# Rows of scales by a DRAM store and a broadcast load in place of a matmul with ones

## The chip, the cores and the metric

The kernel runs on one core of one Trainium2 chip. Its time is the device time of one execution in microseconds, median over runs of the same kernel on the same chip. Inside a core, TensorE (PE) does matmuls, VectorE (DVE) and ScalarE (ACT) work element by element on 128 partitions, and the queues of SyncE (SP) and GpSimd (POOL) issue the transfers between DRAM and the on-chip memory. Each queue is in order: an instruction that waits holds all that stands behind it on the same queue.

## The reference

One encoder layer for two token groups that share the weights: the "sample" (1024 tokens) and the "prompt" (512 tokens), width 2048. Cut to what matters here:

```python
h = rms_norm(x, norm_g)                 # x * rsqrt(mean(x*x) + eps) * g, one scale for each token
z = h @ w_in                            # combined projection, 5632 columns
c_val, c_glu, c_gate, q, k, v, a_gate = split(z)
u = depthwise_conv31(c_val * sigmoid(c_glu)) + b_dw
u = silu(layer_norm(u, ln_g, ln_b))     # (u - mean) * rsqrt(var + eps): one scale for each token
conv_out = (u @ w_pw) * silu(c_gate)    # the "pointwise" product
attn_out = banded_attention(rope(q), rope(k), v, sink) * silu(a_gate)
y = rms_norm(x + concat(conv_out, attn_out) @ w_out, final_norm_g)
```

All is float32. On the chip a token's values lie along one row (the free direction), and the channels lie on the partitions. A scale for each token is therefore needed as a row of 512 numbers that is the same in all 128 partitions, while the sums that it comes from arrive as columns: 512 tokens stand as a tile of 128 partitions by 4.

## The kernel before

Every product runs as float32 split into a high and a low part (three matmuls for each block of 128x128 weights and 512 tokens). The sample's input and output projections use seven products of half-size blocks in place of eight (class `Unit` and `Onto`, line 207); the prompt's projections and both pointwise products are plain (`Job`, line 670). Each `Job` or `Unit` loads 512 KB weight blocks on SP (`raw`), ACT and DVE split them into `hl` (lines 510, 511, or 418, 420 where the low part comes from DRAM), and PE multiplies. At most three `raw` and three `hl` tiles exist.

Side work is written as generators that are queued on three lanes (`conv`: the taps of the convolution; `attn`: attention; `prep`: everything that prepares a later product). After each group of three matmuls the lanes are given `3 * MM` = 648 ns of credit times their rate. A generator does a step, and the number that it yields is the credit that must be earned before its next step. A `yield 6000` is thus a pause of ten groups of three matmuls when the rate is 1, which it is for the `prep` lane at the four places of the change. `drain` and `until` run a lane's remaining steps at once. The compiler layer below orders the instructions of each engine by priority and by the times that it estimates, so an instruction's place on its queue follows from the place at which it is written, from its priority and from that estimate.

Between column and row stands `Encoder.spread` (lines 726 to 743). It splits the 128x4 columns into high and low (lines 731, 732), builds two 128x512 tiles with four scaled copies of the identity each (line 737, eight instructions on DVE), pauses S8 = 6000, and sums over the partitions with two matmuls against a 128x128 tile of ones (line 742). The caller then copies the result from PSUM on ACT. It is used at eight places in time:

- twice in `spread_rms` (sample's RMS scale) and twice in `Mix.finish` (final norm of the sample);
- once in `scale_ahead`: the prompt's RMS scale `rcol`, computed by `rms_ahead` just before with a pause of 15000 behind it. The row `r` then multiplies the prompt's input (line 928), which goes to DRAM as `xr_d` and is loaded much later by `load_two`, when the prompt's projections begin;
- once in each of three `Post.prepare`: two for the halves of the sample's tokens, one behind the other on the `prep` lane, followed by `fetch` of the first half, and one for the prompt (`LastPost`). The scale `r` of the layer norm comes from `column_sums` and `rsqrt` (lines 701 to 724, then a pause S7 = 6000); its row `rs` multiplies the tiles (line 1489), then a SiLU (line 1492). The halves store the result to `cs_d` (line 504) and `fetch` loads it again (line 1513) and splits it (line 510, tile `t<-f`); the prompt's half keeps it and `split` does the same in the last `Onto` unit.

The tile `rs` is `bc[:, 1]` of a T1 tile (F tile for the prompt); `r` of `scale_ahead` is one of four G tiles. The two diagonal tiles of `spread` are two of the four U tiles.

Of the kernel before, what the change touches and what calls it, by code (L numbers as in the profile page):

```python
# [7 lines left out]
F32 = mybir.dt.float32  # L8
F32R = mybir.dt.float32r
AF = mybir.ActivationFunctionType  # L10
# [3 lines left out]
P = 128  # L14
# [25 lines left out]
LOAD = 4500  # L40
LEAD = 9000
SPREAD = 3
RATES = (0.4, 0.6, 0.3, 1.0, 0.5)
S1, S2, S3, S4, S5, S6, S7, S8 = 5000, 6000, 9000, 7000, 3500, 2500, 6000, 6000
NF, NA, NG, NU, NP = 7, 4, 4, 4, 4
# [385 lines left out]
class Encoder:  # L431
# [284 lines left out]
    def rsqrt(self, out, v, b):  # L716
# [6 lines left out]
        nc.vector.tensor_scalar(t, t, -0.5, 1.5, ALU.mult, ALU.add)  # L723
        nc.vector.tensor_tensor(out, s, t, ALU.mult)

    def spread(self, cols, b=NB, room=None):

        nc = self.nc
        hi = self.work.tile([P, b], F32R, tag="tinyr", bufs=4, name=self.name("tinyr"))
        lo = self.small(b)  # L730
        nc.vector.tensor_copy(hi, cols)
        nc.vector.tensor_tensor(lo, cols, hi.bitcast(F32), ALU.subtract)
        parts = []
        for part in (hi.bitcast(F32), lo):
            dg = (room or self.U)([b * P], F32R)
            for j in range(b):
                nc.vector.tensor_scalar(dg[:, j * P : (j + 1) * P], self.ident, part[:, j : j + 1], None, ALU.mult)
            parts.append(dg)
        yield S8
        ps = self.PS("s", [b * P])  # L740
        for n, dg in enumerate(parts):
            nc.tensor.matmul(ps, self.ones_r, dg, start=n == 0, stop=n == 1)
        return ps


class Sequence:
# [169 lines left out]
    def scale_ahead(self):  # L916

        e, nc = self.e, self.e.nc
        ps = yield from e.spread(self.rcol)
        r = e.G()  # L920
        nc.scalar.activation(r, ps, AF.Copy)
        yield 3000
        for i, dst in enumerate(self.xr_d):
            t = e.F([2, self.T])
            nc.sync.dma_start(t, self.xT[2 * i : 2 * i + 2].rearrange("k p t -> p k t"))
            yield 3000
            for j in range(2):
                nc.vector.tensor_tensor(t[:, j], t[:, j], r, ALU.mult)
            e.store(dst, t)
            yield 1500  # L930
# [507 lines left out]
class Post:  # L1438
# [9 lines left out]
    def prepare(self):  # L1448
        e, nc, seq, t0, N = self.e, self.e.nc, self.seq, self.t0, self.N
        cols = slice(t0, t0 + N)  # L1450
        bc, vs = self.room(), self.room()
        mu, rs, va = bc[:, 0], bc[:, 1], vs[:, 0]
        sq = (bc[:, 1], vs[:, 1])
        pairs = []
        for i in range(0, NC, 2):
            t = self.room()
            for j in (0, 1):
                nc.sync.dma_start(t[:, j], seq.conv_d[i + j][:, cols])
            pairs.append(t)
        xc = [pairs[i // 2][:, i % 2] for i in range(NC)]  # L1460
        both = lambda row: row.unsqueeze(1).broadcast_to([P, 2, N])
        yield 2 * LOAD
        nc.vector.tensor_tensor(vs, pairs[0], pairs[1], ALU.add)
        for t in pairs[2:]:
            nc.vector.tensor_tensor(vs, vs, t, ALU.add)
            yield 1500
        nc.vector.tensor_tensor(va, va, vs[:, 1], ALU.add)
        yield S3
        ps = yield from e.sums(va)
        nc.scalar.activation(mu, ps, AF.Copy, scale=1.0 / C)  # L1470
        yield 1000
        for i, t in enumerate(pairs):
            nc.vector.tensor_tensor(t, t, both(mu), ALU.subtract)
            for j in (0, 1):
                n = 2 * i + j
                nc.scalar.activation(sq[j] if n else va, t[:, j], AF.Square)
                if n:
                    nc.vector.tensor_tensor(va, va, sq[j], ALU.add)
            yield 2500
        yield S3  # L1480
        v = e.column_sums(va, N, 1.0 / C, LN_EPS)
        r = e.small(NB)
        e.rsqrt(r, v, NB)
        yield S7
        ps = yield from e.spread(r)
        nc.scalar.activation(rs, ps, AF.Copy)
        yield 1000
        for i, t in enumerate(pairs):
            nc.vector.tensor_tensor(t, t, both(rs), ALU.mult)
            for j in (0, 1):  # L1490
                n = 2 * i + j
                nc.scalar.activation(t[:, j], t[:, j], AF.Silu, scale=e.ln_g[:, n : n + 1], bias=e.ln_b[:, n : n + 1])
            self.normed(i, t)
            yield 3000
# [380 lines left out]
def encoder(ctx, tc, a):  # L1875
# [103 lines left out]
    def pace(unit, rate, lane=e.conv):  # L1979
        unit.before.append(lambda: setattr(lane, "rate", rate))  # L1980
# [9 lines left out]
    rms = sample.spread_rms()  # L1990
    for step in range(SPREAD):
        stages[0][-1].after.setdefault(step, []).append(lambda: e.urgently(next, rms, None))

    pace(stages[1][0], RATES[0])
    pace(stages[2][0], RATES[1])
    pace(stages[3][0], RATES[2])

# [47 lines left out]
    pace(end, 0.0)  # L2045
    pace(pj[2], RATES[3])

# [4 lines left out]
    def prepare():  # L2052
# [5 lines left out]
        for group in prompt.groups:  # L2058
            e.attn.add(group)

    pj[PM].before.append(prepare)
    pace(pj[PM], RATES[4])
    jobs = sum(items, []) + [[j] for j in pj]
# [114 lines left out]
```

## Time and profile before

| | us |
|---|---|
| median of 3 runs | 2078.28 (2077.58 to 2078.65) |
| profiled execution, its own time | 2079.13 |
| its span in the profile | 2077.4 |
| PE busy | 2060.1 |
| DVE busy | 1728.4 |
| ACT busy | 1081.8 |
| mean granted TensorE clock | 0.998 |

The span is the time between the first and the last instruction in the trace; the execution's own time is 1.73 us longer. "Busy" is the time in which the engine had at least one instruction under way. In the rows of a timeline the columns are the start in us, the length in us, the engine, the source line, the operation, the tiles written and read, and how many instructions were merged into the row; in square brackets stands the idle time before it and what ended it. In the chain of waits a row is start, length, and the engine and line on which the end depended at that time.

### The profile page before, as it was taken

What the parts mean: (1) busy time and instruction counts of PE and PEld (TensorE: products, weight loads), DVE (VectorE), ACT (ScalarE), POOL (GpSimd) and SP (SyncE); (2) the same over time, 40 slices, a digit from 0 to 9 for tenths busy, and PEclk for the clock granted to TensorE, in tenths of its full rate; (3) what the DMA queues carried; (4) which work ended last, traced back from release to release, by engine and by line L of the source; (5) the groups of instructions that cost most, each with busy time, mean ns of one, the idle gap of its engine ahead of it and who ended that gap; (6) DMA issues with size and microseconds to landing.
All of it is one profiled execution on the core that took longest, in us unless ns stands there. A gap on an engine that the chain in (4) does not pass through costs nothing.

```text
span 2077.4 us, 27223 instructions
## 1 busy us (share of the span) xinstructions
PE 2060.1 (99%) x9256; PEld 1697.9 (82%) x9256; DVE 1728.4 (83%) x2843; ACT 1081.8 (52%) x1771; POOL 157.9 (8%) x240
## 2 busy tenths in 40 slices
PE   9999999999999999999999999999999999999998
PEld 8888888888888888788888888888888887888886
DVE  8768899998899899889766777776799978998877
ACT  7486445333465555655555777336553343454454
POOL 0111111111112111100000000000000111100000
PEclk9999999999999999999999999999999999999999
DMA  8888886864577777954555555997789898778897
GB/s 285 309 300 256 200 215 226 286 218 158 190 243 197 181 167 179 279 167 158 164 183 185 178 172 188 316 329 233 239 295 295 279 324 283 213 259 277 293 324 279
DMA packets 242300, 494.56 MB, mean 238 GB/s; under 512 B 23664, under 2 KB 84464, under 8 KB 242160
## 3 DMA queue, kind: packets, MB, share of 16 engines
q1 hardware_dynamic: 216352, 428.83, 62.1%
q0 software_dynamic: 24512, 61.88, 12.5%
q10 hardware_dynamic: 1296, 2.11, 0.3%
q8 instruction: 72, 1.18, 0.2%
q14 instruction: 68, 0.56, 0.1%
HBM read 331.77 MB, written 160.96 MB: 237 GB/s over the span
## 4 chain that ended last, share of the span: by engine, by line
PE 73%; issue 8%; DMA 8%; DVE 7%; ACT 2%; POOL 1%; SPq 0%; ACTq 0%; POOLq 0%; DVEq 0%
PE a L207 21%; PE a L670 13%; PE c L207 10%; PE b L670 6%; PE c L670 6%; PE b L207 5%; PE s L1169 2%; PE pv L1198 2%; PE a L1852 2%; PE s L207 2%; DVE hl L511 2%; PE pt L1203 1%; PE s L1852 1%; DVE t L511 1%; DMA p<-y_d 1%
## 5 line engine op out<-in xcount | busy, mean ns | idle before, releaser
L207 PE MATMUL a<-t,hl 128*128 128x512 f32 x2640 | 632.5, 390 | 1.8 <-ACT u L236 1.3
L207 PEld LDWEIGHTS a<-t,hl 128*128 128x128 f32 x2640 | 493.5, 188 | 108.4 <-ACT u L236 2.4
L511 DVE TENSOR_TENSOR hl<-raw,hl 128x1024 fp32r<-128x1024 f32 (+3 forms) x334 | 337.8, 1012 | 151.5 <-ACT hl L510 147.3
L510 ACT ACTIVATE hl<-raw 128x1024 fp32r<-128x1024 f32 (+3 forms) x334 | 296.8, 889 | 314.4 <-PE c L207 88.1
L670 PE MATMUL a<-t,hl 128*128 128x512 f32 x1344 | 326.3, 393 | 0.0
L207 PE MATMUL c<-t,hl 128*128 128x512 f32 x1320 | 319.1, 389 | 0.0
L670 PEld LDWEIGHTS a<-t,hl 128*128 128x128 f32 x1344 | 248.8, 188 | 50.4
L207 PEld LDWEIGHTS c<-t,hl 128*128 128x128 f32 x1320 | 247.4, 188 | 51.5 <-DVE u L304 0.2
L1041 DVE SCALAR_TENSOR_TENSOR f<-f,c_w_dw,f 128x512 f32<-128x512 f32 x248 | 172.9, 744 | 0.2
L670 PE MATMUL b<-t,hl 128*128 128x512 f32 x672 | 162.9, 392 | 1.5 <-DVE t L515 0.8
L670 PE MATMUL c<-t,hl 128*128 128x512 f32 x672 | 163.9, 393 | 0.0
L1004 DVE SCALAR_TENSOR_TENSOR f<-f,c_w_dw,f 128x512 f32<-128x512 f32 x232 | 163.4, 742 | 0.2
L207 PE MATMUL b<-t,hl 128*128 128x512 f32 x660 | 159.8, 389 | 0.0
L670 PEld LDWEIGHTS b<-t,hl 128*128 128x128 f32 x672 | 124.8, 188 | 27.5 <-DVE t L515 1.1
L670 PEld LDWEIGHTS c<-t,hl 128*128 128x128 f32 x672 | 124.6, 188 | 24.8
L207 PEld LDWEIGHTS b<-t,hl 128*128 128x128 f32 x660 | 123.7, 188 | 25.6
L1033 DVE SCALAR_TENSOR_TENSOR f<-f,w_both,f 128x512 f32<-128x512 f32 x120 | 89.8, 748 | 2.0
L236 ACT ACTIVATE u<-a 128x512 f32<-128x512 f32 x82 | 48.8, 595 | 77.3 <-PE a L207 70.6
L236 ACT ACTIVATE g<-a 128x512 f32<-128x512 f32 x78 | 46.5, 596 | 78.5 <-PE a L207 68.5
L1183 ACT ACTIVATE p<-p,tiny 128x384 f32<-128x384 f32 (+1 forms) x96 | 54.6, 570 | 45.9 <-DVE tiny L1180 36.2
L510 ACT ACTIVATE a<-pt 128x512 fp32r<-128x512 f32 x64 | 38.0, 593 | 64.6 <-PE pt L1203 64.4
L285 POOL DMA_DIRECT2D g<-xT_s x16 | 8.8, 551 | 743.1 <-DMA att_d<-u 669.0
(356 smaller groups left out, 2765.2 us busy)
## 6 DMA issues: line engine op xcount, KB each, us to landing
raw<-w_in SPq DMA_DIRECT2D x170, 512.0 KB, 5.2
raw<-w_out SPq DMA_DIRECT2D x31, 512.0 KB, 5.1
raw<-w_pw SPq DMA_DIRECT2D x24, 512.0 KB, 4.2
wsum_P<-raw SPq DMA_DIRECT2D x47, 256.0 KB, 3.6
raw<-wsum_P SPq DMA_DIRECT2D x18, 512.0 KB, 5.1
f<-x_s SPq DMA_DIRECT2D x16, 512.0 KB, 8.5
g<-wsum_P SPq DMA_DIRECT2D x28, 256.0 KB, 4.6
a<-sum_S SPq DMA_DIRECT2D x24, 256.0 KB, 6.1
```

What stands on the lines that cost most here:

```text
L207: nc.tensor.matmul(acc, hl[:, l, o, j, :], toks[j][:, r], start=name in FRESH and j == 0 and q == 0, stop=name in LAST and j == HALF - 1 a ...
L236: nc.scalar.activation(t, bank, AF.Copy)
L510: nc.scalar.activation(hi, x, AF.Copy)
L511: nc.vector.tensor_tensor(lo, x, hi.bitcast(F32), ALU.subtract)
L670: nc.tensor.matmul(job.acc[0], hl[:, l, kk // HALF, kk % HALF, :], r, start=i == 0 and p == 0, stop=i == nk - 1 and p == 2,)
L1004: nc.vector.scalar_tensor_tensor(t, h[:, j : j + T], w(j), t, ALU.mult, ALU.add)
L1033: nc.vector.scalar_tensor_tensor(m0, odd[:, j : j + H], both(j), m0, ALU.mult, ALU.add)
L1041: nc.vector.scalar_tensor_tensor(out, d[:, j : j + H], w(2 * j + k), out if j else m0, ALU.mult, ALU.add)
L1169: nc.tensor.matmul(ps[:, 0:n], qs[:, x, h], k[y][:, keys], start=p == 0, stop=p == 2)
L1183: nc.scalar.activation(p[:, 0:n], p[:, 0:n], AF.Exp, bias=nm[:, h : h + 1], accum_out=l[:, h : h + 1])
L1198: nc.tensor.matmul(pv, v[x][:, vs], pt[:, y], start=i == 0 and p == 0, stop=i == last and p == 2)
L1852: nc.tensor.matmul(acc[t], self.toks[name, m][:, x, i, t * P : (t + 1) * P], parts[i][l].rearrange("p a b -> p (a b)"), start=fresh and fi ...
```

## The change

A new method `spread_far` takes a destination tile and the columns. It stores the 128x4 columns to a DRAM row of 512 numbers, pauses FAR = 6000, loads the row back into all 128 partitions with one broadcast transfer, and pauses FAR again. Both transfers are issued on SP. Two callers use it: `scale_ahead` (once) and `Post.prepare` (three times). In both the split, the eight scaled identities, the pause S8, the two matmuls and the copy from PSUM are gone. In `scale_ahead` the G tile is now taken ahead of the store. `spread_rms` and `Mix.finish` keep `spread`.

```diff
+FAR = 6000
...
+    def spread_far(self, dst, cols):
+        b = cols.shape[1]
+        row = self.tc.dram_tile([1, b * P], F32, name=self.name("row"))
+        self.store(row.rearrange("o (j p) -> p (o j)", p=P), cols)
+        yield FAR
+        self.nc.sync.dma_start(dst, row.broadcast_to([P, b * P]))
+        yield FAR
...
     def scale_ahead(self):
 
         e, nc = self.e, self.e.nc
-        ps = yield from e.spread(self.rcol)
         r = e.G()
-        nc.scalar.activation(r, ps, AF.Copy)
+        yield from e.spread_far(r, self.rcol)
         yield 3000
...
         e.rsqrt(r, v, NB)
         yield S7
-        ps = yield from e.spread(r)
-        nc.scalar.activation(rs, ps, AF.Copy)
+        yield from e.spread_far(rs, r)
         yield 1000
```

## The prediction

> **What bounds the kernel.** I read the page's busy line first, then busy time by stretch for PE alone, then PE's own waits.
>
> ```profile
> PE 2060.1 (99%) x9256; PEld 1697.9 (82%) x9256; DVE 1728.4 (83%) x2843; ACT 1081.8 (52%) x1771; POOL 157.9 (8%) x240
> core 0: us, PE busy (x), PEclk, DMA share, GB/s
> 350.00:420.00 70.00, 70.00 (x311) 1.00 0.74 259
> 1160.00:1300.00 140.00, 139.93 (x662) 1.00 0.57 185
> 1300.00:1420.00 120.00, 118.73 (x532) 1.00 0.89 308
> 1420.00:1800.00 380.00, 378.64 (x1716) 1.00 0.84 276
> 1800.00:1860.00 60.00, 60.00 (x269) 1.00 0.75 239
> sum 2077.40, PE 2060.05; mean PE 257.51
> ```
>
> PE is busy for all but 17.3 us of the span. The three stretches in which the change lies (350 to 420, 1160 to 1300, 1800 to 1860) hold 0.07 us of idle PE between them, at the full granted clock. So what the change takes off PE is time won, one for one, and what it takes off other engines is worth nothing unless PE waits for them. From 1160 to 1860 PE idles 0.07 + 1.27 + 1.36 = 2.70 us; more than that can't be won there by better feeding.
>
> **The matmuls that go.** Four of the eight calls of `spread` go, two matmuls each. The chain of waits runs over PE at three of the places and gives each matmul's share of the path; at the third place the PE timeline does.
>
> ```profile
> 359.56 2.72 PE b L207 x12
> 371.13 0.46 PE s L742 x2
> 1180.06 0.23 PE s L742
> 1181.55 0.24 PE s L742
> 1280.11 0.62 PE L742 MATMUL s<-u,ones_r 128*128 128x512 f32 x2
> 1280.57 0.86 PE L670 MATMUL c<-t,hl 128*128 128x512 f32 x3
> 1819.34 0.23 PE s L742
> 1820.03 0.29 PE s L742
> ```
>
> They cost 0.46 + 0.23 + 0.24 + (1280.57 - 1280.11 = 0.46, the 0.62 being overlapped by the next) + 0.23 + 0.29 = 1.91 us. An ordinary matmul of the same shape takes 2.72 / 12 = 0.227, and eight of them 1.81. I take the middle, 1.85 us. This is the only term with a sure place on the path.
>
> **DVE and ACT work that goes.** For each place two small instructions and eight scaled identities on DVE, one copy on ACT:
>
> ```profile
> 1270.47 0.16 DVE L731 CAST tinyr<-tiny 128x4 fp32r<-128x4 f32 x1
> 1270.67 0.88 DVE L737 TENSOR_SCALAR u<-c_ident,tinyr 128x128 fp32r<-128x128 f32 x4
> L1486 ACT ACTIVATE t<-s x2: 577/587/597, 1181.8 to 1281.1; 128x512 f32<-128x512 f32 x2
> ```
>
> The two DVE rows come once for the high and once for the low part: 2 x (0.16 + 0.88) = 2.08 us of DVE and 0.59 of ACT, 8.3 and 2.4 over the four. The stretches above show PE full there, so I cost this gain at nothing. Its upper bound is the 0.07 us idle in them; with later stretches, the third rival.
>
> **What is added on SP: the store.** It waits for the last instruction of `rsqrt`, as line 731 did before. What then stands behind it on SP are weight loads and stores. When `r` was ready in the first place and in the last, and the first instruction of the old `spread` in the first:
>
> ```profile
> 350.32 0.16 DVE L724 TENSOR_TENSOR stat<-tiny,tiny 128x4 f32<-128x4 f32 x1
> 364.59 0.16 DVE L731 CAST tinyr<-stat 128x4 fp32r<-128x4 f32 x1
> 1812.28 0.17 DVE L720 RECIPROCAL tiny<-tiny 128x4 f32<-128x4 f32 x1
> 1816.06 0.16 DVE L724 TENSOR_TENSOR tiny<-tiny,tiny 128x4 f32<-128x4 f32 x1
> SPq L504 <- DVE hl L511: 28.1, 7, 11.0
> ```
>
> In the first place `r` is 14 us early and SP waits for nothing. In the last one DVE put other work into `rsqrt`, which ran from 1812.28 to 1816.22; if SP gets there when that chain begins, it waits 3.9 us. The last row (SP's waits from 360 to 425) says what such a wait is worth: SP stood 11.0 us at one store, in a stretch in which PE lost nothing. So: 0 taken, and PE's loss is bounded by the slack of the weights, below.
>
> **The load.** It waits until the store has landed. Ahead of it lies a pause of 6000, ten ticks of three matmuls, 10 x 3 x 0.227 = 6.8 us. No transfer of before writes 4-byte pieces. The nearest rows of the issues (line, KB, median us to landing):
>
> ```profile
> wsum_P<-raw SPq DMA_DIRECT2D x47, 256.0 KB, 3.6
> xr_d<-f SPq DMA_DIRECT2D x8, 512.0 KB, 7.1
> a<-msum_S SPq DMA_DIRECT2D x12, 256.0 KB, 6.7
> ```
>
> `wsum_P<-raw` writes 128 partitions x 4 pieces of a 512-wide row, the store's pattern of 512 pieces with more bytes in each: 3.6 us. The slowest store is 7.1. I take 3.6 as the nearest, so the load finds it landed; at 7.1 SP stands 0.3 us. The load brings 256 KB into 128 rows like `a<-msum_S`, a slow one of its size: 6.7 us, under the second pause of 6.8 us, so DVE finds its row there; the 1000 or 3000 of credit that follow are kept besides.
>
> **What moves.** At each place two pauses of 6000 replace one, so the rest of the `prep` lane is written 6000 (6.8 us) later, after both halves' preparation 12000 (13.6 us, more where attention fills in). Who needs it, and when:
>
> ```profile
> L928 DVE TENSOR_TENSOR f<-f,g x16: 672/674/683, 380.3 to 422.2; 128x512 f32<-128x512 f32 x16
> L2015 SPq DMA_DIRECT2D a<-xr_d x6: 319/320/327, 605.5 to 846.3; - x6
> 1341.42 1.16 ACT L510 ACTIVATE t<-f 128x512 fp32r<-128x512 f32 x2 [4.48 <-DMA f<-cs]
> 1436.00 5.61 PE L670 MATMUL b<-t,hl 128*128 128x512 f32 x24
> 1838.14 1.51 ACT L1492 ACTIVATE f<-f,c_conv_ln_b,c_conv_ln_g 128x512 f32<-128x512 f32 x2
> 1848.77 0.61 ACT L510 ACTIVATE t<-f 128x512 fp32r<-128x512 f32 x1
> 1866.64 5.60 PE L670 MATMUL b<-t,hl 128*128 128x512 f32 x24
> ```
>
> The prompt's scaled input is finished about 7 us after 422 and loaded from 605.5 on. The sample's first half is split by 1342, then by about 1356; its first matmul is at 1436. The tightest is the prompt: its last SiLU ends at 1839.65, then at 1846.5, its split begins at 1848.77 and its first pointwise matmul at 1866.64. That leaves 2.3 us to the split and 18 to PE. All costed at 0 for this reason. The G tile held some 12 us longer and the two U tiles freed at each place stand against each other; PE's fullness hides both.
>
> **Sum.** The profiled execution took 2079.13 (span 2077.4 and 1.73 around it), 0.85 above the median. Less 1.85 it is 2077.28; on the median 2078.28 - 1.85 = 2076.4. The new order of the queues will move PE's few idle places by some tenths either way. I say 2076.5, 0.09% below before; a measurement of this kernel can tell about 0.2% (4.2 us) from no change, so this is "the same".
>
> **First rival: later traffic in a full stretch.** From 1300 to 1420 the DMA share is 0.89 at 308 GB/s, and PE already loses 1.27 us there:
>
> ```profile
> f<-cs SPq DMA_DIRECT2D x8, 512.0 KB, 5.9
> 1373.95 6.69 DVE f L1004 x11
> 1383.44 5.97 DMA a<-ag_d
> ```
>
> DVE works off eleven taps in a row, a gate of the attention lands late, and the operands of the next scores are late behind both. The change moves loads and stores of `cs` (512 KB each, 524288 / 308000 = 1.7 us of all engines) 13.6 us later into that stretch. For it: only 0.57 of the DMA is busy in the stretch that they leave. Against: they are 1 to 3 transfers, spread over 50 us. One to three in the way of that chain give 2078.2 to 2081.6.
>
> **Second rival, the slow side: SP stands at the load.** If 512 single-number pieces land far later than 3.6 us, SP stands at the load's wait and the weights come late. How long PE is covered, at the third place:
>
> ```profile
> 1280.57 1.22 DVE L511 TENSOR_TENSOR hl<-raw,hl 128x1024 fp32r<-128x1024 f32 x1 [2.79 <-DMA raw<-w_in]
> 1285.95 1.55 PE L670 MATMUL a<-t,hl 128*128 128x512 f32 x6
> DMA to landing us min/median/max: 3.7/5.6/9.1
> ```
>
> The `hl` for the job that starts at 1285.95 is ready at 1281.79, 4.2 us of slack. PE pays from a landing of 6.8 + 4.2 = 11 us on, which exceeds the slowest weight load around (9.1). At twice that, 18.2 us, SP stands 11.4, PE loses 7.2 at a place: 2083.7 for one, 2090.9 for two. Against it stand all rows of stores above.
>
> The Trainium skill, in "DMA: Bandwidth & Descriptors", speaks for this rival: "Rules for kernel authors" says that a last dimension that isn't contiguous becomes one descriptor for each element, and "Specifications" that pieces under 512 B are done as read-modify-write. By that rule the store's 4-byte pieces could each cost more than the 512-byte ones of `wsum_P<-raw`; by the row they cost no more. No run here shows 4-byte writes.
>
> **Third rival: the feeding gets better too.** With DVE relieved and the order changed, the idle time behind the second place, 2.70 us, may go as well: 2076.4 - 2.7 = 2073.7. Against: none of the waits there names the work that is removed.
>
> **How the numbers follow.** My forecast (2075.0 to 2078.2) 62%, the first rival 17%, the second 10%, the third 11%. Faster by over 0.2% means below 2074.1: nearly all of the third rival, 0.10. Slower by over 0.2% means above 2082.4: the second and a small part of the first that comes with more transfers, 0.12. The rest, 0.78, lies between. The range reaches from a little below the third rival, 2073.0, to the edge of the first, 2082.0; it leaves out the second.
>
> **What would show it.** Line 742 with 8 matmuls in place of 16, PE's busy time lower by about 1.8 and its idle time near 17.3. The store's landing near 3.6 us and no long wait of SP for the row. Lines 928 and 1489 without idle DVE ahead of them. `t<-f` of the first half near 1356 and the prompt's last SiLU near 1846. I am wrong if SP's waits show the row with more than 4 us at a place, if PE's idle time from 1300 to 1420 grows, or if it falls below 15 us in all.

## The result, and the profile after

The changed kernel takes 2104.81 us, median of 4 runs (2101.38 to 2107.92), against 2077.93 (2075.00 to 2078.65) before: the ratio is 1.013, with a 95% interval of 1.0113 to 1.0146. It is 27 us slower; 2076.5 was forecast. The profiled execution took 2107.08 us with a span of 2105.3.

The line of busy times of the changed kernel, and its busy time of PE by stretch (columns: stretch, its length, PE busy with the number of matmuls, granted clock, DMA share, GB/s):

```profile
PE 2067.0 (98%) x9248; PEld 1701.2 (81%) x9248; DVE 1723.3 (82%) x2803; ACT 1079.5 (51%) x1767; POOL 157.6 (7%) x240
```

```profile
350.00:420.00 70.00, 70.00 (x311) 1.00 0.82 255
1160.00:1300.00 140.00, 134.47 (x628) 0.98 0.54 152
1300.00:1440.00 140.00, 131.17 (x563) 0.96 0.88 301
1440.00:1820.00 380.00, 377.08 (x1712) 1.00 0.84 276
1820.00:1880.00 60.00, 53.60 (x230) 0.94 0.71 191
1184.00:1192.00 8.00, 2.47 (x10) 0.81 0.66 198
1192.00:1196.00 4.00, 4.00 (x14) 0.53 0.70 216
1856.00:1860.00 4.00, 0.34 (x1) 0.74 0.70 218
1860.00:1864.00 4.00, 4.00 (x10) 0.50 0.73 236
1864.00:1868.00 4.00, 4.00 (x17) 0.90 0.44 140
```

The eight matmuls are gone (9256 to 9248), and yet PE is busy 6.9 us longer, and the span is 27.9 longer. So there are two losses. PE's idle time rose from 2077.4 - 2060.1 = 17.3 to 2105.3 - 2067.0 = 38.3, by 21.0. And PE's busy time rose by 6.9 although 1.85 us of work left it, so that the same matmuls took 8.75 us longer. The last five rows show how: behind each gap the granted clock is 0.5 for a while.

The idle time sits at three places, none of them the first one (350 to 420 is full): 5.53 us up to 1300, 8.83 from 1300 to 1440, 6.40 from 1820 to 1880. Before, these stretches and the one from 1440 to 1820 had 0.07, 1.27, 0 and 1.36.

What SP, DVE and PE waited for in the changed kernel (engine, line, what it waited for: us in all, times, longest):

```profile
SPq L732 <- DMA row<-tiny: 27.8, 3, 11.5
```

```profile
DVE t L1496 <- DMA t<-row: 9.1, 2, 7.1
DVE f L1496 <- DMA f<-row: 6.6, 1, 6.6
```

```profile
PE a L208 <- DVE u L305: 6.9, 2, 6.4
PE pv L1206 <- DVE a L512: 5.9, 2, 5.5
PE s L1177 <- ACT a L511: 3.6, 1, 3.6
```

Line 732 is the broadcast load, 1496 the first multiplication by the loaded row. PE names neither: its longest waits are for DVE work of attention (512) and of the output projection (305); the 3.6 us for line 511 lie in the stretch from 1300 on. The link is in the chain of waits at the second and the fourth place (start, length, what), and in DVE's and PE's timelines:

```profile
1171.77 12.68 DMA row<-tiny
1184.47 4.92 DMA t<-row
1189.41 0.06 DVE t L1496
1190.56 0.70 DVE a L512
1191.30 1.22 PE pv L1206 x2
1836.12 11.65 DMA row<-tiny
1847.84 3.95 DMA f<-row
```

```profile
1189.41 1.23 DVE L1496 TENSOR_TENSOR t<-t,t 128x1024 f32<-128x1024 f32 x1 [7.15 <-DMA t<-row]
1851.81 1.23 DVE L1496 TENSOR_TENSOR f<-f,f 128x1024 f32<-128x1024 f32 x1 [6.61 <-DMA f<-row]
```

```profile
1191.30 1.22 PE L1206 MATMUL pv<-a,t 128*128 128x512 f32 x2 [5.53 <-DVE a L512]
1859.66 5.36 PE L208 MATMUL a<-t,hl 128*128 128x512 f32 x12 [6.40 <-DVE u L305]
```

The store of 512 single numbers lands after 12.68 and 11.65 us. SP issues the load only then, the load takes 4.9 and 3.95, and DVE, which goes through its instructions in order, stands 7.15 and 6.61 us in front of the multiplication. Behind it on DVE stood work that PE needed. And the twelve matmuls at 1859.66 took 5.36 us, where the prediction showed 2.72 for twelve.

### The profile page after: what moved, and what is told of

It reads as the page before. It is cut to its first block, busy times and chain, and to the rows that moved or that the text cites. A ratio compares the mean times of both kernels' runs of the same rounds, so it can differ in the third digit from the quotient of the medians.

```text
span 2105.3 us, 27176 instructions
## 1 busy us (share of the span) xinstructions
PE 2067.0 (98%) x9248; PEld 1701.2 (81%) x9248; DVE 1723.3 (82%) x2803; ACT 1079.5 (51%) x1767; POOL 157.6 (7%) x240
## 4 chain that ended last, share of the span: by engine, by line
PE 73%; DMA 8%; issue 8%; DVE 7%; ACT 2%; POOL 1%; SPq 0%; ACTq 0%; POOLq 0%; DVEq 0%
PE a L208 20%; PE a L671 11%; PE c L208 10%; PE c L671 6%; PE b L671 5%; PE b L208 5%; PE s L1177 2%; PE pv L1206 2%; PE s L1859 2%; DMA a<-ag_d 2%; PE a L1859 2%; PE s L208 2%; DVE hl L512 2%; PE pt L1211 1%; DMA row<-tiny 1%
## 5 line engine op out<-in xcount | busy, mean ns | idle before, releaser
L671 PEld LDWEIGHTS b<-t,hl 128*128 128x128 f32 x672 | 126.1, 190 | 27.9 <-DVE t L516 1.1
L512 DVE TENSOR_TENSOR a<-pt,a 128x512 fp32r<-128x512 f32 x64 | 44.0, 688 | 33.0 <-ACT a L511 32.2
```

Source lines behind the costliest of these rows:

```text
L512: nc.vector.tensor_tensor(lo, x, hi.bitcast(F32), ALU.subtract)
L671: nc.tensor.matmul(job.acc[0], hl[:, l, kk // HALF, kk % HALF, :], r, start=i == 0 and p == 0, stop=i == nk - 1 and p == 2,)
```

## The experiments

Each kernel was run alternately with the kernel before on the same chip. The theories, with a letter each: shift (S), the later writing of the `prep` lane alone; queue (Q), SP stands at the load and what is behind it comes late; DVE (D), DVE stands in order at the row; contention (C), the store of tiny pieces holds up the core's other transfers; order (O), the new order of instructions by itself. S and O have nothing to do with the transfers' lengths, Q, D and C have. In the expectations W stands for Q and D together, and O3 for O at the second half alone.

| run | edit | us | ratio (95%) |
|---|---|---|---|
| e1 | only the first place changed | 2076.56 | 0.9993 (0.9984 to 1.0003) |
| e3 | before, with the pause alone | 2076.94 | 0.9992 (0.9981 to 1.0004) |
| e2 | load doesn't wait for the store | 2084.07 | 1.0032 (1.0022 to 1.0042) |
| e4 | both pauses 16000 | 2077.22 | 0.9997 (0.9986 to 1.0008) |
| e5 | both transfers on POOL's queue | 2107.44 | 1.0143 (1.0126 to 1.0160) |
| e7 | second pause 16000 | 2085.63 | 1.0044 (1.0027 to 1.0061) |
| e8 | only the prompt's preparation | 2086.11 | 1.0043 (1.0028 to 1.0058) |
| e12 | all but the second half's | 2092.29 | 1.0081 (1.0064 to 1.0098) |
| e14 | only the second half's | 2089.94 | 1.0054 (1.0036 to 1.0072) |
| e15 | e14 without store | 2080.22 | 1.0008 (0.9998 to 1.0018) |
| e9 | before, with four unused stores | 2077.88 | 1.0005 (0.9995 to 1.0014) |
| e10 | before, with one unused store | 2078.28 | 1.0010 (1.0000 to 1.0020) |
| e13 | e3 with four unused stores | 2084.85 | 1.0025 (1.0015 to 1.0035) |
| e6 | store of 128 pieces of 16 bytes | 2090.05 | 1.0060 (1.0044 to 1.0077) |
| e11 | store of 4 pieces of 512 bytes | 2084.21 | 1.0031 (1.0017 to 1.0044) |
| e16 | e11 with both pauses 16000 | 2077.07 | 0.9996 (0.9985 to 1.0006) |

### Which places, and is it the shift?

e1 keeps the old way in `Post.prepare`. e3 keeps the old way everywhere and only gives `spread` a pause of 12000 at the four places:

```diff
-        yield S8
+        yield pause          # 2 * S8 at the four places of the change
```

> Only scale_ahead goes by the store and the load; the three Post.prepare keep the matmuls. Theory W (the wait: the store lands after 9 to 13 us, the load stands behind it on SP, the first multiplication stands behind the load on DVE, and PE runs dry): the place at 350 has three other SP instructions' worth of work and 14 us between store and load and no PE idle in the changed kernel, so no loss: 2075 to 2079, one PE pair (0.46 us) gained. Theory S (shift: the prep lane's later place in the order costs the time, whatever carries the row): nothing is shifted after 1160, so 2075 to 2079 too. Theory O (any new order of the queues costs some 10 us in this kernel): 2085 to 2100.

> The kernel before with the matmul way, but with the pause of 6000 made 12000 at the four places, which moves the prep lane as the change does. Theory W: no new wait, 2076 to 2081. Theory S: most of the 27 us, 2095 to 2108. Theory O: anything up to 2100.

Both are level with before. The first place costs nothing, and the later writing costs nothing: S is out, and so is the thought that the preparations come too late by 6.8 us.

### SP's queue or DVE's?

e4 sets `FAR = 16000`. e5 issues both transfers with `gpsimd.dma_start`, so that SP never waits for the row. e7 leaves the pause between store and load at 6000 and makes only the one behind the load 16000. e8 uses `spread_far` only for the prompt's `Post.prepare`.

> The changed kernel with FAR = 16000 in place of 6000, so that each pause is 18 us of matmuls. Theory W: the store has landed when the load's turn comes, if the longer pause also puts more work between the two on SP; the 5.5 and 6.4 us of idle PE go, 2076 to 2086. Theory S: a larger shift, slower than the changed kernel, 2105 to 2125; and a deadline at the last product may be passed, which would show as idle PE at about 1850 to 1870.

> The changed kernel with both transfers of spread_far issued on POOL's queue in place of SP's, pauses of 6000 as in the change. Three theories for the 27 us. Q (SP stands at the load for up to 11.5 us and the weights behind it come late): SP is free, so 2075 to 2082. D (the first multiplication by the row stands at the head of DVE's queue until the load has landed, and PE's operands stand behind it): DVE waits for the row as before, 5 to 9 us at the first half and at the prompt, 2092 to 2108. C (while the 512 single numbers are written, every transfer of the core is held up, whichever queue it is on): some loss stays from 1280 to 1440 whatever DVE does, 2082 to 2108.

> The changed kernel with the pause behind the load made 16000, the one ahead of it 6000 as in the change. SP stands at the load as long as in the change; only the multiplications are written later: on DVE's queue the first one moves by 18 instructions at the prompt, by 3 only at the first half. D: the 6.4 us idle at the prompt and the half clock behind it go, those at the first half mostly stay: 2082 to 2096. Q: nothing changes, 2098 to 2108. C: the part from 1280 to 1440 may stay: 2084 to 2100.

> Only the prompt's Post.prepare goes by the store and the load; scale_ahead and the two halves keep the matmuls. D: the wait of DVE at the prompt (6.6 us), the 6.4 us of idle PE behind it and 3.4 us for the half clock that follows: 2084 to 2090. If the whole loss hangs on the stretch from 1280 to 1440: 2076 to 2079.

e5 is as slow as the change. SP is free there, and DVE stands still longer, so that a gain from the freed queue could hide behind it:

```profile
DVE t L1496 <- DMA t<-row: 16.1, 2, 8.9
DVE f L1496 <- DMA f<-row: 9.3, 1, 9.3
```

And while the store on POOL's queue is under way, from 1174.6 and from 1834.8 on, the transfers of SP's queue hardly move (the last two columns are DMA share and GB/s):

```profile
1182.00:1186.00 4.00, 4.00 (x23) 1.00 0.31 19
1838.00:1842.00 4.00, 4.00 (x20) 1.00 1.13 59
```

e4 loses nothing, and yet SP stands 21.3 us at the load, at the first half and at the prompt, the two places of the long gaps. DVE doesn't wait for the row at all. SP's wait, then PE by stretch:

```profile
SPq L732 <- DMA row<-tiny: 21.3, 2, 10.7
```

```profile
1160.00:1300.00 140.00, 140.00 (x662) 1.00 0.62 186
1304.00:1308.00 4.00, 4.00 (x19) 1.00 0.87 59
1300.00:1440.00 140.00, 138.05 (x621) 1.00 0.89 298
1820.00:1880.00 60.00, 60.00 (x266) 1.00 0.82 236
```

In e7 SP stands longest of all, and DVE shorter:

```profile
SPq L732 <- DMA row<-tiny: 33.6, 3, 11.7
```

```profile
DVE t L1496 <- DMA t<-row: 3.8, 2, 2.3
DVE f L1496 <- DMA f<-row: 0.7, 1, 0.7
```

The prompt's loss is gone in e7 (PE 60.00 of 60 from 1820 to 1880); what it still loses, 8.7 us, lies at the two halves (137.03 of 140 up to 1300, 134.82 of 140 behind). In e8 the prompt's place alone shows the whole of mechanism D, with a store of 12.23 and a load of 3.58 us in its chain, DVE's wait of 6.8 and this gap:

```profile
1816.04 12.23 DMA row<-tiny
1828.28 3.58 DMA f<-row
```

```profile
1839.74 5.23 PE L208 MATMUL a<-t,hl 128*128 128x512 f32 x12 [6.56 <-DVE u L305]
```

```profile
1820.00:1856.00 36.00, 29.44 (x121) 0.91 0.68 159
```

The clock of 0.91 over 36 us is (1 - 0.91) / 0.5 x 36 = 6.5 us at half speed, worth 3.2 at most. So 6.56 + 3.2 - 0.5 for the two matmuls saved = 9.3; measured are 2086.11 - 2076.97 = 9.1. D holds. Q is out at these two places by e4, where SP's standing costs nothing; that freeing SP gains nothing in e5 agrees with it.

### The loss that remains: the second half

D explains the gaps at 1191 and 1859. It does not explain the 8.83 us from 1300 to 1440, where DVE stood only 1.9 us at the row. In e12 only the second half's `Post.prepare` goes the old way, in e14 only it goes the new way. e2 keeps all stores, but the load reads an input row, so that it waits for none of them. e15 is e14 with such a load and no store.

> All four places as in the change, the stores too, but each load reads a row of an input (the final gain) in place of the stored row, so it waits for no store; the scales that are multiplied are therefore not the ones computed. Pauses, shifts, number and size of transfers and the missing matmuls stay. Theory W: the loss goes, 2074 to 2080, and SP's waits for the row and DVE's idle time ahead of the first multiplication (15.7 us in the changed kernel) are gone. Theory S: it stays, 2098 to 2108. Theory O: 2085 to 2108.

> The changed kernel with the matmul way at the second half alone. C: the stretch from 1300 to 1440 loses 1 to 2 us in place of 8.8; the idle PE at the first half (5.5 us and the half clock behind it) and at the prompt (6.4 us and the half clock) stays: 2094 to 2099. If the stretch's loss comes from the first half's lateness or from the shift: 2101 to 2107.

> Only the second half goes by the store and the load (pauses of 6000); the first half, the prompt and scale_ahead keep the matmuls. Both theories: idle PE from 1300 to 1440 of 4 to 9 us, no loss elsewhere, 2082 to 2090. If the loss needs the first half's lateness too (its row at 1189): 2076 to 2080.

> As the run with the second half alone, but without the store, and the load reads a row of an input, which is always there; the scale multiplied at that half is therefore not the one computed. C: nothing holds up the transfers, 2076 to 2079. O3: the order is the same as with the store, so 2080 to 2085.

e12 keeps the losses at the first half (PE 133.69 of 140 up to 1300) and at the prompt (54.27 of 60) and has 139.12 of 140 from 1300 to 1440: that loss hangs on the second half. (Its 2092.29 us are a little under the 2094 to 2099 expected.) In e14 the place shows D once more, with a longer wait (DVE 10.3 us at the row, PE idle 6.5 behind it, up to 1289); from 1300 to 1440 PE idles 3.3 us there, less than both theories expected. In e2 neither DVE nor SP waits for a row, and 6.2 us are still lost, more than W expected and less than S; the profiled execution has its idle PE in the stretch behind the second half (133.95 of 140, against 139.95 and 60.00 in the other two). Something beside D is at work there.

The next three kernels have the matmuls of before and read nothing back: the store's only effect can be on other transfers and on SP. e9 stores at all four places just ahead of `spread`, e10 at the second half alone, and e13 adds e3's pause, which moves the store 12 us later in the stretch, to where it is in e2:

```diff
+    def also_store(self, cols):
+        b = cols.shape[1]
+        row = self.tc.dram_tile([1, b * P], F32, name=self.name("row"))
+        self.store(row.rearrange("o (j p) -> p (o j)", p=P), cols)
...
+        e.also_store(self.rcol)
         ps = yield from e.spread(self.rcol)
```

> The kernel before, matmuls and all, with the four stores of 512 single numbers added just ahead of each spread; nothing reads them, so no load stands at a store and no multiplication waits for a row. Theory C (a store of 512 single numbers holds up every transfer of the core for 8 to 10 us; only where the transfers are full afterwards, from 1280 to 1400, can it not be made up): under 60 GB/s for some 6 us behind each store, no loss at the first, second and fourth place, idle PE of 2 to 6 us from 1300 to 1440 in place of 1.3: 2079 to 2085. Without C: 2076 to 2079.

> The kernel before with one such store added, at the second half (about 1280). C: all of the loss of the four stores hangs on this one, so the same time as with the four within 2 us, and the same idle PE from 1300 to 1440. Without C: 2076 to 2079.

> The kernel before with the matmuls, the pause of 12000 at the four places and the four stores of 512 single numbers that nothing reads. The second half's store then comes near 1280 in place of 1270. If the loss is a store's hold-up at the edge of the full stretch (theory C with its time): 2080 to 2085 and 3 to 6 us idle PE from 1300 to 1440. If it is the new order of the queues (theory O3: with the matmuls gone the second half's multiplications and stores are placed differently): 2076 to 2079.

e9 and e10 showed no loss that the runs can tell, against what C expected of them, and e13 lost 6.6 us. The second half's store is issued at 1269.28 in e9 and at 1281.10 in e13. PE and DMA around it, in before, e9 and e13 in that order:

```profile
1280.00:1300.00 20.00, 19.93 (x92) 1.00 0.80 277
1300.00:1440.00 140.00, 138.73 (x623) 1.00 0.87 298
```

```profile
1272.00:1276.00 4.00, 4.00 (x19) 1.00 1.02 117
1276.00:1280.00 4.00, 4.00 (x20) 1.00 0.80 26
1280.00:1284.00 4.00, 3.93 (x19) 1.00 0.87 299
1300.00:1440.00 140.00, 139.52 (x628) 1.00 0.87 299
```

```profile
1284.00:1288.00 4.00, 4.00 (x22) 1.00 0.84 45
1288.00:1292.00 4.00, 4.00 (x19) 1.00 0.38 33
1300.00:1440.00 140.00, 134.29 (x594) 0.99 0.86 304
```

For 4 to 8 us nearly nothing moves: 26 to 45 GB/s, at a DMA share of up to 0.84. e3 has the same order as e13 without the stores, and moved 406 and 282 GB/s in e13's two stretches. Its transfers issued from 1280 to 1293 landed after 3.4 to 5.9 us in the median of each kind; e13's took 8.7 to 13.8. In e13 SP itself is held up with it, at an issue that takes 0.43 us in the median of line 1308 of the changed kernel, the same transfer:

```profile
1286.74 5.76 SPq L1306 DMA_DIRECT2D a<-att_d  x1
```

In e9 that time lies ahead of 1280, where the DMA had room to spare (its share was 0.46 from 1260 to 1280 before), and it is made up by 1300. In e13 it lies in the first microseconds of the full stretch, and PE's first gap ends at 1342.5. So C holds, and it cost time where the DMA was full right behind it. The same hold-up from 1300 on in e4 (the row with 59 GB/s above) costs nothing, so a full DMA alone doesn't decide.

The chains name the late transfer: the gate of the attention, `a<-ag_d`, at which DVE stands in order as it does at the row. Two rows of the changed kernel's chain, and what DVE did at the first of them:

```profile
1311.21 7.71 DMA a<-ag_d
1399.41 8.23 DMA a<-ag_d
```

```profile
1318.94 1.23 DVE L1313 TENSOR_TENSOR a<-a,a 128x1024 f32<-128x1024 f32 x1 [5.74 <-DMA a<-ag_d]
```

PE stood 2.33 and 1.26 us up to 1329 behind the first, for weights that ACT and DVE split late, and 3.58 us up to 1410 behind the second, for scores. In e13 such a gate landed after 10.54 us, at 1337, and the gap up to 1342.5 is behind it. This is read from the chains; no run took the gate out. DVE waits for gates in the kernel before too (20.4 us from 1300 to 1440), and PE idles only 1.27 us there, so the length of these waits alone doesn't say what they cost.

e15, without a store, is 1.9 us over before, with an interval from 0.9998 to 1.0018, at the low edge of what O3 expected: what the changed order costs there is at most 3.7 us, and may be nothing.

### The size of the pieces

e6 stores the columns as 128 pieces of 16 bytes, and DVE reads the row permuted. e11 transposes the columns on PE to four rows, so that the store has 4 pieces of 512 bytes; e16 is e11 with `FAR = 16000`.

```diff
-        self.store(row.rearrange("o (j p) -> p (o j)", p=P), cols)
+        ps = self.PS("s", [P])
+        self.nc.tensor.transpose(ps[0:b, :], cols, self.ident)
+        t = self.U([P])
+        self.nc.scalar.activation(t[0:b, :], ps[0:b, :], AF.Copy)
+        self.store(row.rearrange("o (j p) -> (o j) p", p=P), t[0:b, :])
```

> The changed kernel with the row stored in the order 4p + j, so that the store is 128 pieces of 16 bytes in place of 512 of 4; the multiplications read the row permuted (twice as many at Post.prepare, half as long). Order of the queues, pauses and waits are otherwise the same. Theories D and Q alone: if the landing depends on the number of pieces, it falls from 9 to 13 us to 4 to 6, DVE's wait for the row (9.1 and 6.6 us) to 0 to 2, and the time to 2076 to 2084. C: the stretch after a store in which the core moves under 60 GB/s falls from 8 to 10 us to 2 to 4, the same times. If a store of pieces under 512 bytes is slow however many they are: landing 9 us and more, 2095 to 2108.

> The changed kernel with the 128x4 columns turned to 4x128 by a small transpose on PE and a copy on ACT, so that the store is 4 pieces of 512 bytes in place of 512 of 4; pauses 6000. D and C: the store lands in 2 to 4 us, the core's transfers go on behind it, DVE does not wait for the row, idle PE from 1300 to 1440 under 2 us: 2075 to 2080. If the round trip over DRAM is too long whatever the pieces, 2090 and more; if the new order from 1280 to 1440 costs by itself, 2080 to 2086.

> The row turned to 4x128 on PE and stored in 4 pieces of 512 bytes, with FAR = 16000. No theory sees a wait or a hold-up here; what the order costs is what is left. C: 2075 to 2079, as with FAR = 16000 and 512 pieces (2077.2). O3: 2077 to 2084.

With larger pieces SP's wait shrinks; e6 first, then e11:

```profile
SPq L732 <- DMA row<-tiny: 9.9, 2, 5.4
```

```profile
SPq L736 <- DMA row<-u: 3.9, 1, 3.9
```

DVE's wait for the row is 0.4 us in e6 and 3.4 in e11. The loss is 13 us in e6, half of the change's, and 7 in e11; in e16 it is gone. e6's 13 us lie between its expectations, and they don't price the pieces alone: a permuted multiplication took 1.09 us where one of twice the width takes 1.22, so DVE spent 26.2 us on them at `Post.prepare`, where the changed kernel spends 14.6. Most of the idle PE that it adds is from 1300 to 1440 again (133.97 of 140). e11's is not settled: its runs spread from 2077.63 to 2088.77, and the profiled one, at 2078.82, shows little of it (137.18 of 140); its median lies where a cost of the new order was expected, and nothing here rules that out. None of the versions beats the kernel before by more than the runs can tell: e1, e3, e4 and e16 are level with it.

## Why the prediction was wrong

**Right.** The matmuls: line 742's 16 became 8, and PE was full at the places, so 1.85 us of work left it; no run is fine enough to show a gain of this size. The first place costs nothing (e1). The shift of the lane costs nothing (e3). e4 and e16, where DVE never stands at the row, end where the sum did: level with before.

**The store, "I take 3.6 as the nearest".** This is the step that failed. The four stores landed after 9.0, 12.7, 9.2 and 11.7 us. The row `wsum_P<-raw` had the same number of pieces, but 512 bytes in each; the bound of 7.1 from the slowest store was a bound by bytes, and the number of small pieces wasn't in it. The sentence on the Trainium skill beside the second rival pointed the right way: in "DMA: Bandwidth & Descriptors" ("Rules for kernel authors", "Specifications") one descriptor for each element, and read-modify-write below 512 bytes. The runs agree in kind: 512 pieces of 4 bytes landed after 9 to 13 us, 128 of 16 bytes after 1.4, 6.4, 4.3 and 4.9, and for 4 of 512 bytes SP stood 3.9 us at one place and nowhere else.

**The pause as time, "so the load finds it landed".** Credit decides when an instruction is written, not what lies ahead of it on its engine's queue. Between store and load SP had none to three other instructions at the three later places, and it came to the load while the store was still under way: 11.5 us of waiting at the longest, where the prediction allowed 0.3. At the first place it had eight, and that one costs nothing.

**"DVE finds its row there".** What stands behind the row on DVE was never costed: the text followed only SP and the weights. The row came 12.68 + 4.92 = 17.6 us after the store's issue at the first half and 15.6 at the prompt, where the sum had 3.6 + 6.7 = 10.3. DVE stood 7.1 and 6.6 us, and PE's cover there was 7.1 - 5.5 = 1.6 and 6.6 - 6.4 = 0.2, not 4.2.

**The second rival** had the cause, 512 pieces that land late, and 10%. Its path was wrong (weights behind SP; Q), and so was its price: 7.2 us for one place, 14.4 for two. e8 measured 9.1 for one. The rest lies in a term that no case had.

**The clock.** Behind these gaps PE runs at half clock. (A stretch's share of lost clock, over 0.5 and times its length, is its time at half clock.) By the rows of 1184 to 1196 it lasted 0.19 / 0.5 x 8 + 0.47 / 0.5 x 4 = 6.8 us, by those of 1856 to 1868 2.1 + 4 + 0.8 = 6.9. From 1300 to 1440 the mean of 0.96 gives 0.04 / 0.5 x 140 = 11.2, in two pieces. That is 25 us at half speed, some 5 of them while PE still stood; the other 20 are worth half of that, some 10 us, not far from the 8.75 us of longer matmuls. The Trainium skill, in "TensorE: Matmul & The Clock Gate" ("What's actually happening"), says that the clock halves after an idle window of about 3.4 us and comes back after as long a busy one. The gaps of 5.5 and 6.4 us agree with the first; half speed held for some 4.5 and 5 us of work behind them, a little longer than the second says. Shorter gaps than that window were enough, too: behind 2.45 us without a matmul in e14 (up to 1405) and 2.81 in e15 (up to 1395) the clock was at half for 3.4 us each; behind 1.70 us in e13 (up to 1342.5) it stayed full.

**The hold-up of the transfers** (C) wasn't foreseen. "Later traffic in a full stretch" looked at the right stretch, from 1300 on, with the wrong traffic: not the `cs` transfers that come later, but those that the store keeps back. The path that this rival described, a gate that lands late, DVE behind it and the next scores late, is the one in the changed kernel's chain; it had 17%, and at most 5.1 us for what cost 7.6 us of idle PE and the half clock behind it.

Together: 21.0 us of idle PE (5.46 at the first half, 7.56 and 1.56 behind the second, 6.40 at the prompt), 8.75 of slow matmuls, less 1.85, are the 27.9 of the span. The prediction named two of its own signs of error, SP's wait for the row above 4 us and more idle time from 1300 on; both came.

## What to carry to other kernels

Cost a store to DRAM by its pieces, not its bytes, and add the whole round trip (here 15 to 18 us for 2 KB at the three places where the load came next or nearly so) before the engine that reads the result. A pause in the order of writing is worth only the instructions that it puts on the waiting engine's own queue: ask for each engine in the chain, the reading one above all, what stands behind the wait. Where PE is full, count the slow matmuls behind a gap as well: here gaps of 2.5 to 6.6 us were followed by 3.4 to 6.9 us at half clock, which cost another 1.6 to 2.6 us each by the traces.

## What the runs showed of the hardware

- 2 KB stored in 4-byte pieces landed after 9 to 13 us, and for 4 to 8 us of it the core's other transfers all but stood still (19 to 59 GB/s in the stretches shown, where 94 to 406 moved in the same stretches of the kernel before or of e3), also those of another queue (e5). An issue on SP took 5.76 us meanwhile.
- The broadcast of the same 2 KB into 128 rows landed after 3.9 to 6.1 us, like other loads.
- After 5.5 and 6.4 us without a matmul the granted clock was 0.5 for 6.8 and 6.9 us, beginning before PE did; after 2.45 (e14) and 2.81 us (e15) it was 0.5 for 3.4 us.
